# Second FFN of a one-layer diffusion block: gate and up as a 2x2 block product with seven products in place of eight

## The chip, the cores and the metric

One core of one Trainium2 chip runs the whole layer as a single launch. Every time is in device microseconds. A run's time is that of one execution; the profile comes from one execution of its own, and its clock starts with the span. The five engines work through instruction lists of their own, in order, and meet through semaphores: PE (TensorE, matmuls into PSUM; PEld are its weight loads), DVE (VectorE), ACT (ScalarE), POOL (GpSimd) and SP, which here only issues DMAs.

## What is computed

The layer takes 1024 latent tokens and 256 context tokens of width 1024. It is a half-step SwiGLU, a mixer (latent attention beside a state-space scan) and a second half-step SwiGLU, then a final RMSNorm. The change touches the second SwiGLU, which runs on the latent tokens alone:

```python
def swiglu(h, w_gu, w_down):
    gate, up = jnp.split(h @ w_gu, 2, axis=-1)
    return (jax.nn.silu(gate) * up) @ w_down
...
x = x + mx[5] * mix_x
x = x + 0.5 * mx[8] * swiglu(modulate(x, g_ffn2[l], mx[6], mx[7]), w_gu2[l], w_down2[l])
return rmsnorm(x, g_final)
```

`w_gu2` is 1024 x 5632 (gate and up, 2816 columns each), `w_down2` is 2816 x 1024.

## The kernel before

All matrix products are made in three passes: each operand is split into a rounded high part H (ACT copies it to the matmul type) and a remainder L (DVE or POOL subtracts), and `mm3` (L621 to L623) issues H·H, H·L and L·H into one PSUM bank. A matmul is 128 x 128 weights against 512 columns.

`mix_out_ffn2` (L1564) first makes the mixer's output projection, token tile by token tile (eight of 128), and then calls `ffn`. `ffn` walks f over 22 slices of 128 hidden columns. The 1024 tokens form two blocks of 512, `hT[0]` and `hT[1]`, kept transposed (eight k tiles of 128 on partitions). In step f it makes gate of both blocks (2 x 24 matmuls, tag `gu`), then the down product of slice f-1 (eight token tiles x two halves x 3 matmuls = 48, tag `dn`), each half added by DVE to the residual stream `acc` (L62, a helper that records every tensor_tensor), then up of both blocks (2 x 24). SiLU (L720) is ACT's, the product with up is DVE's, its split ACT's and POOL's. So a step has 144 matmuls and 16 additions of a PSUM bank to `acc`.

PSUM has four banks for `gu` and four for `dn`. Weights come by SP's queue (L663): gate and up of a slice are 128 x 1024 each, down 128 x 1024; they share four raw buffers. DVE multiplies down by the broadcast gate `g8`, ACT and POOL split all three (1024 wide). The order of work on every engine is the order in which the code is written; nothing reorders it. With `joint`, the down products of the last two slices are held back and made together, tile by tile, six matmuls into a bank; after each tile comes its share of the final norm: sum of squares on ACT, `rstd` (DVE, then a power on POOL), a scaled copy on DVE and the store.

The first slice's gate and up weights are loaded and split during the projection (L1690 to L1697). The normed tokens of block 1 (`xn`, tiles 4 to 7) are ready only after the last projection tile; their transposes (`trans(1, ...)` through `hook`) run between the matmuls of f = 0 on block 0.

Of the kernel before, what the change touches and what calls it, by code (L numbers as in the profile page):

```python
# [7 lines left out]
F32 = mybir.dt.float32  # L8
F32R = mybir.dt.float32r
# [38 lines left out]
class Kernel:  # L48
# [1515 lines left out]
    def mix_out_ffn2(self, sbig):  # L1564
        nc, a, acc = self.nc, self.a, self.acc
        B2 = [(0, 4), (4, 4)]
        with ExitStack() as st:
# [3 lines left out]
            P = {"w": w2}  # L1571
            xp = self.pool(st, "xn", bufs=4)
            with ExitStack() as s1:
# [113 lines left out]
                pre0 = {}  # L1687
                for t in range(2, NX):
                    if t in (2, 4):
                        which = t // 2 - 1  # L1690
                        wr = sm.tile([128, D], F32, tag="wor", name="w2r")
                        nc.sync.dma_start(wr, a["w_gu2"][0, which].rearrange("p k f -> p (k f)"))
                    if t in (3, 5):
                        pre0[0, which] = [tuple(w2.tile([128, 1024], F32R, tag=f"w{x}{which}", name=f"w{x}{which}")
                                                for x in "HL")]
                        self.split(wr, *pre0[0, which][0], nc.gpsimd)
# [11 lines left out]
            P["sg"], P["nsg"] = self.pool(st, "sg2"), 3  # L1708
            fin = self.pool(st, "fin2")
            g8 = fin.tile([128, D], F32, name="g8")  # L1710
            gf = fin.tile([128, D], F32, name="gf")
            self.gate_bc(g8, (8, 0))
            nc.sync.dma_start(gf, a["g_final"].to_broadcast([128, D]))
            P["gates"] = [(g8, P["act"])]
            out = self.out.rearrange("(j s) d -> j s d", s=NX)

            def hook(b):
                todo = list(range(KT if b else 0))

                def pre(kt):  # L1720
                    while todo and todo[0] <= kt + 2:
                        trans(1, todo.pop(0), "dn")
                return pre

            down = self.ffn(B2, hT, a["w_gu2"], a["w_down2"], acc, P, hook, preload=pre0, keep=True, joint=True)
            S = {}

            def post(t, cs, p):
                self.tt(acc[t][:, cs], p, acc[t][:, cs], ADD)

            def final(t):
                R = self.rstd(S.pop(t), D, "n")
                for q in range(2 if t == NX - 1 else 1):
                    cs = slice(q * 512, q * 512 + 512) if t == NX - 1 else slice(0, D)
                    self.stt(J[t][:, cs], acc[t][:, cs], R, gf[:, cs], MUL, MUL)
                    nc.sync.dma_start(out[:, t, cs], J[t][:, cs])

            J = {}
            for t in range(NX):
                down([t], post)  # L1740
                J[t] = xp.tile([128, D], F32, tag="xn", name="j")
                S[t] = self.sumsq(acc[t], J[t], "n")
                if t:
                    final(t - 1)
            final(NX - 1)


# [77 lines left out]
```

## Time and profile before

| what | value |
|---|---|
| three timed runs | 2544.89, 2546.02 (median), 2550.65 us |
| the profiled execution's own time | 2544.01 us |
| its span | 2542.2 us |
| PE busy in the span | 2427.4 us (95%) |
| DVE / ACT / POOL busy | 1434.2 / 816.1 / 1036.1 us |
| second FFN in the span | about 1803 to 2542 us |

How to read it: rows of the timeline give the start, the time from the first start to the last end, the engine, the line, the operation with output and inputs, a count, and in brackets the idle time before them with what ended it. Busy matmuls overlap (each is shown 0.39 us long, but one starts every 0.23 us), so a rate is taken from starts. PEclk is the granted TensorE clock, 1.00 at 2.4 GHz and 0.50 at 1.2 GHz.

### The profile page before, as it was taken

How to read it: one execution, taken by the hardware profiler on the slowest of the kernel's cores; microseconds unless marked ns; L12 is line 12 of the kernel's file. 1: busy time of each engine (PE TensorE's matmuls, PEld its weight loads, DVE VectorE, ACT ScalarE, POOL GpSimd, SP SyncE). 2: the span in 40 equal slices, each digit the busy share in tenths (PEclk: the TensorE clock that was granted, in tenths of full speed). 3: DMA queues.
4: the chain of work that ended last, by engine and by line, in shares of the span. 5: the costliest groups of instructions: out<-in, count | busy, mean ns of one | idle time of the engine just before them, and what ended most of it. 6: DMA issues, size and time to landing. Idle time of an engine off the chain costs nothing. (4 is left out here: it accounts for less than half of the span.)

```text
span 2542.2 us, 31980 instructions
## 1 busy us (share of the span) xinstructions
PE 2427.4 (95%) x12100; PEld 2004.9 (79%) x12100; DVE 1434.2 (56%) x2480; ACT 816.1 (32%) x1570; POOL 1036.1 (41%) x947
## 2 busy tenths in 40 slices
PE   7999998999999999898999999999999999999998
PEld 4788777888888887787777777777788888888886
DVE  3667578345434537747788888863344444444443
ACT  4311211211121112533677777762411111111112
POOL 2422314433433333426576666755433223323222
PEclk9999999999999999899999999999999999999999
DMA  7234621222222123316000000113211111111111
GB/s 283 86 106 135 205 83 38 71 70 59 75 71 71 57 79 126 123 38 192 23 17 4 14 14 25 38 66 126 75 44 49 50 50 50 50 45 46 50 42 67
DMA packets 83544, 185.14 MB, mean 73 GB/s; under 512 B 22199, under 2 KB 41911, under 8 KB 82366
## 3 DMA queue, kind: packets, MB, share of 16 engines
q1 hardware_dynamic: 59990, 163.93, 19.3%
q10 hardware_dynamic: 23400, 19.16, 2.6%
q8 instruction: 95, 1.56, 0.3%
q14 instruction: 59, 0.48, 0.1%
HBM read 155.52 MB, written 27.54 MB: 72 GB/s over the span
## 5 line engine op out<-in xcount | busy, mean ns | idle before, releaser
L62 POOL TENSOR_TENSOR wL<-raw,wH 128x1024 fp32r<-128x1024 f32 x130 | 313.8, 2418 | 787.6 <-ACT wH L616 776.5
L62 DVE TENSOR_TENSOR acc<-dn,acc 128x512 f32<-128x512 f32 x516 | 350.4, 690 | 352.3 <-PE dn L623 352.1
L621 PE MATMUL gu<-big,wH 128*128 128x512 f32 (+1 forms) x1056 | 379.9, 360 | 3.0 <-ACT sg L720 1.5
L623 PE MATMUL gu<-big,wL 128*128 128x512 f32 (+1 forms) x1056 | 374.8, 355 | 2.3 <-POOL wL L62 2.3
L622 PE MATMUL gu<-big,wH 128*128 128x512 f32 (+1 forms) x1056 | 374.6, 355 | 1.8 <-POOL big L62 1.8
L621 PE MATMUL dn<-wH,aH 128*128 128x512 f32 x792 | 314.6, 397 | 18.9 <-DVE acc L62 14.1
L623 PE MATMUL dn<-wH,aL 128*128 128x512 f32 x792 | 311.3, 393 | 1.0 <-POOL aL L62 1.0
L622 PE MATMUL dn<-wL,aH 128*128 128x512 f32 x792 | 311.4, 393 | 0.0
L616 ACT ACTIVATE wH<-raw 128x1024 fp32r<-128x1024 f32 x130 | 136.3, 1055 | 497.9 <-DVE raw L62 226.5
L62 DVE TENSOR_TENSOR sg<-gu,sg 128x512 f32<-128x512 f32 (+1 forms) x110 | 69.8, 635 | 391.7 <-PE gu L623 369.6
L622 PE MATMUL gu<-hL,wH 128*128 128x512 f32 x704 | 274.5, 390 | 4.3 <-POOL hL L62 3.0
L621 PE MATMUL gu<-hH,wH 128*128 128x512 f32 x704 | 274.6, 390 | 0.0
L623 PE MATMUL gu<-hH,wL 128*128 128x512 f32 x704 | 273.9, 389 | 0.0
L62 POOL TENSOR_TENSOR aL<-sg,aH 128x512 fp32r<-128x512 f32 (+1 forms) x110 | 140.4, 1277 | 277.5 <-ACT aH L616 275.0
L621 PEld LDWEIGHTS gu<-big,wH 128*128 128x128 f32 x1056 | 200.1, 189 | 36.0 <-issue 4.1
L623 PEld LDWEIGHTS gu<-big,wL 128*128 128x128 f32 x1056 | 199.9, 189 | 31.5 <-POOL wL L62 3.4
L622 PEld LDWEIGHTS gu<-big,wH 128*128 128x128 f32 x1056 | 200.1, 189 | 31.1 <-POOL big L62 2.2
L616 ACT ACTIVATE aH<-sg 128x512 fp32r<-128x512 f32 (+1 forms) x110 | 64.7, 589 | 461.6 <-DVE sg L62 425.0
L621 PEld LDWEIGHTS dn<-wH,aH 128*128 128x128 f32 x792 | 150.5, 190 | 54.4 <-DVE acc L62 15.8
L62 DVE TENSOR_TENSOR ptL<-pt,ptH 128x512 fp32r<-128x512 f32 x240 | 162.8, 686 | 52.2 <-ACT ptH L1417 51.7
L623 PEld LDWEIGHTS dn<-wH,aL 128*128 128x128 f32 x792 | 150.6, 190 | 33.6 <-POOL aL L62 1.4
L622 PEld LDWEIGHTS dn<-wL,aH 128*128 128x128 f32 x792 | 150.9, 191 | 31.1 <-issue 0.5
(317 smaller groups left out, 4635.7 us busy)
## 6 DMA issues: line engine op xcount, KB each, us to landing
raw<-in_w_gu SPq DMA_DIRECT2D x86, 512.0 KB, 3.4
wmr<-in_w_mod SPq DMA_DIRECT2D x56, 512.0 KB, 4.5
raw<-in_w_down SPq DMA_DIRECT2D x44, 512.0 KB, 3.3
row<-d_s SPq DMA_DIRECT2D x16, 576.0 KB, 4.0
wm<-in_w_mod SPq DMA_DIRECT2D x8, 1024.0 KB, 7.1
d_s<-T ACTq DMA_DIRECT2D x32, 160.0 KB, 2.7
ck<-d_s SPq DMA_DIRECT2D x16, 320.0 KB, 4.0
acc<-in_x SPq DMA_DIRECT2D x8, 512.0 KB
```

Source lines behind the costliest of these rows:

```text
L62: (eng or self.nc.vector).tensor_tensor(out=out, in0=a, in1=b, op=op)
L616: self.nc.scalar.activation(out=H, in_=raw, func=AF.Copy)
L621: mm(out, lhsT=AH, rhs=BH, start=start, stop=False)
L622: mm(out, lhsT=AH, rhs=BL, start=False, stop=False)
L623: mm(out, lhsT=AL, rhs=BH, start=False, stop=stop)
```

## The change

For one slice f the products of gate and up form a 2x2 block product. The four weight blocks are A11 and A12 (gate weights, k tiles 0-3 and 4-7) and the blocks a21 and A22 (up weights, the same halves). The four token blocks are B11 and B21 (block 0, k tiles 0-3 and 4-7; they are `hT[0]`) and B12 and B22 (block 1). Seven products of 12 matmuls each (four k tiles x three passes) take the place of eight: A11·B11, A12·B21, S1·T1, S2·T2, S3·T3, S4·B22 and A22·T4. S1 to S4 are sums of weight blocks, made anew for each slice by DVE (`Products.add`); T1 to T4 are sums of token blocks, made once in f = 0 (`part`). The seven banks are combined by DVE into gate and up of both blocks, in four scratch halves of `acc[8]` and `acc[9]` (P1, U2, U3, C22).

The new `ffn2` has a loop of its own. A step's order on PE is A11, S2, S3, S1, the down product of f-1, A12, A22, S4. The sums for slice f+1 and the splits of A11, S2, S3, S1 stand ahead of the down product, those of A12, A22, S4 at the step's end, followed by the loads of gate and up for f+2 (`load_gu`) and of down for f (`load_wd`, with its product by `g8` and its split). Raw buffers are single. The last down product is made alone, not together with the one before.

In the diff, some lines are left out, among them the removed body and the variant of `add` for slice 0 (`sums`), which runs in three parts during projection tiles 3, 4 and 5.

```diff
-            P = {"w": w2}
-            xp = self.pool(st, "xn", bufs=4)
+            raw1 = self.pool(st, "raw1")
+            sx = ExitStack()
+            xp = self.pool(sx, "xn", bufs=4)
+            ops = Products(self, w2)
...
+                    if t == 2:
+                        wr = [sm.tile([128, D], F32, tag="wor", name="w2r"), raw1.tile([128, D], F32, tag="r", name="w2r")]
+                        for which in range(2):
+                            nc.sync.dma_start(wr[which], a["w_gu2"][0, which].rearrange("p k f -> p (k f)"))
+                    if t == 3:
+                        prep = ops.sums(*wr, xp.tile([128, 512], F32, tag="hf", name="s", bufs=2))
+                    if t in (3, 4, 5):
+                        next(prep, None)
...
-                hB = self.pool(st, "hT2b", side="right")
-                hT.append(tuple(hB.tile([128, KT, 512], F32R, name=f"h{x}1") for x in "HL"))
-            P["act"] = P["wd"] = self.pool(st, "act2", bufs=2)
-            P["raw"] = self.pool(st, "raw2", bufs=4)
...
+
+    def ffn2(self, st, sx, h0, ops, raw1, xp, XN):
...
+        B["B11"], B["B21"] = (tuple(h[:, k:k + 4, :] for h in h0) for k in (0, 4))
...
+        def product(p, op, k):
+            (H, L), (bH, bL) = ops[op], B[pair[op]]
+            ks = slice(k * 128, (k + 1) * 128)
+            self.mm3(p, H[:, ks], L[:, ks], bH[:, k, :], bL[:, k, :], k == 0, k == 3)
+
+        def whole(op):
+            p = self.bank("gu", op)
+            for k in range(4):
+                product(p, op, k)
+            return p
+
+        def part(k, tt):
+            f = []
+            for kt, pool, tag in ((k, xp, "hf"), (k + 4, tt, "b22")):
+                t = self.bank("dn", "tp")
+                for i in range(4):
+                    nc.tensor.transpose(t[:, i * 128:(i + 1) * 128], XN[4 + i][:, kt * 128:(kt + 1) * 128], self.ident)
+                x = pool.tile([128, 512], F32, tag=tag, name=tag, bufs=2)
+                nc.scalar.activation(out=x, in_=t, func=AF.Identity, scale=av[:, kt:kt + 1], bias=bv[:, kt:kt + 1])
+                f.append(x)
+            b12, b22 = f
+            t1, t2, t3, t4 = (tt.tile([128, 512], F32, tag=f"t{i}", name=f"t{i}") for i in range(4))
+            g = lambda x, i: B[x][i][:, k, :]
+            fp = lambda x, i: g(x, i).bitcast(F32)
+            self.tt(t1, fp("B11", 0), fp("B11", 1), ADD)
+            self.tt(t4, fp("B21", 0), fp("B21", 1), ADD)
+            self.tt(t1, b12, t1, SUB)
+            self.split(t1, g("T1", 0), g("T1", 1), nc.gpsimd)
+            self.tt(t2, b22, t1, SUB)
+            self.split(t2, g("T2", 0), g("T2", 1), nc.gpsimd)
+            self.tt(t3, b22, b12, SUB)
+            self.split(t3, g("T3", 0), g("T3", 1))
+            self.tt(t4, t4, t2, SUB)
+            self.split(t4, g("T4", 0), g("T4", 1))
+            self.split(b22, g("B22", 0), g("B22", 1), nc.gpsimd)
+
+        wd, act = {}, {}
+        W = {}
+
+        def load_gu(f):
+            if f < NF:
+                r = [raw1.tile([128, D], F32, tag="r", name="rg"), W["raw"].tile([128, D], F32, tag="r", name="ru")]
+                for i in range(2):
+                    nc.sync.dma_start(r[i], a["w_gu2"][f, i].rearrange("p k f -> p (k f)"))
+                W[f] = r
+
+        def load_wd(f):
+            r = W["raw"].tile([128, D], F32, tag="wd", name="wdr")
+            nc.sync.dma_start(r, a["w_down2"][f])
+            self.tt(r, r, g8, MUL)
+            H, L = (W["act"].tile([128, D], F32R, tag=f"wd{x}", name=f"wd{x}") for x in "HL")
+            self.split(r, H, L, nc.gpsimd)
+            wd[f] = (H, L)
+
...
+        def down(f, tiles):
+            for t in tiles:
+                aH, aL = act[f][t // 4]
+                ts = slice((t % 4) * 128, (t % 4 + 1) * 128)
+                for half in range(2):
+                    cs = slice(half * 512, half * 512 + 512)
+                    p = self.bank("dn", "dn")
+                    self.mm3(p, aH[:, ts], aL[:, ts], wd[f][0][:, cs], wd[f][1][:, cs], True, True)
+                    self.tt(acc[t][:, cs], p, acc[t][:, cs], ADD)
+
...
+        for f in range(NF):
+            P1, U2, U3, C22 = tmp
+            if f == 0:
+                with ExitStack() as s1:
+                    tt = self.pool(s1, "tt")
+                    p1, p2 = (self.bank("gu", x) for x in ("A11", "A12"))
+                    for i, (p, op) in enumerate(((p1, "A11"), (p2, "A12"))):
+                        for k in range(2):
+                            part(2 * i + k, tt)
+                            product(p, op, 2 * k)
+                            product(p, op, 2 * k + 1)
+                sx.close()
+                W["act"] = self.pool(st, "act2")
+                W["raw"] = self.pool(st, "raw2")
+                g8 = self.pool(st, "fin2").tile([128, D], F32, name="g8")
+                self.gate_bc(g8, (8, 0))
+                load_gu(1)
+            else:
+                p1 = whole("A11")
+            nc.scalar.copy(P1, p1)
+            self.tt(U2, whole("S2"), P1, ADD)
+            self.tt(U3, whole("S3"), U2, ADD)
+            p = whole("S1")
+            self.tt(C22, p, U3, ADD)
+            self.tt(U2, p, U2, ADD)
+            if f + 1 < NF:
+                ops.add(*W[f + 1], temps)
+                for x in ("A11", "S2", "S3", "S1"):
+                    ops.split(x)
+            if f:
+                down(f - 1, range(NX))
+                p2 = whole("A12")
+            self.tt(P1, p2, P1, ADD)
+            nc.scalar.activation(out=P1, in_=P1, func=AF.Silu)
+            self.tt(U3, whole("A22"), U3, ADD)
+            self.tt(P1, P1, U3, MUL)
+            act[f] = [split_act(0, P1)]
+            self.tt(U2, whole("S4"), U2, ADD)
+            nc.scalar.activation(out=U2, in_=U2, func=AF.Silu)
+            self.tt(U2, U2, C22, MUL)
+            act[f].append(split_act(1, U2))
+            if f + 1 < NF:
+                for x in ("A12", "A22", "S4"):
+                    ops.split(x)
+            load_gu(f + 2)
+            load_wd(f)
+
+        gf = W["raw"].tile([128, D], F32, tag="wd", name="gf")
+        nc.sync.dma_start(gf, a["g_final"].to_broadcast([128, D]))
+        out = self.out.rearrange("(j s) d -> j s d", s=NX)
...
+        def final(t):
+            R, J = self.rstd(S.pop(t), D, "n"), acc[8 + t % 2]
+            for q in range(2 if t == NX - 1 else 1):
+                cs = slice(q * 512, q * 512 + 512) if t == NX - 1 else slice(0, D)
+                self.stt(J[:, cs], acc[t][:, cs], R, gf[:, cs], MUL, MUL)
+                nc.sync.dma_start(out[:, t, cs], J[:, cs])
+
+        for t in range(NX):
+            down(NF - 1, [t])
+            S[t] = self.sumsq(acc[t], acc[8 + t % 2], "n")
+            if t:
+                final(t - 1)
+        final(NX - 1)
...
+    def add(self, g, u, temp):
+        k, half = self.k, lambda x, i: x[:, i * 512:(i + 1) * 512]
+        s = self.src
+        s["A11"], s["A12"], a21, s["A22"] = half(g, 0), half(g, 1), half(u, 0), half(u, 1)
+        s["S1"] = temp()
+        k.tt(s["S1"], a21, s["A22"], ADD)
+        s["S2"] = temp()
+        k.tt(s["S2"], s["S1"], s["A11"], SUB)
+        s["S3"] = a21
+        k.tt(a21, s["A11"], a21, SUB)
+        s["S4"] = temp()
+        k.tt(s["S4"], s["A12"], s["S2"], SUB)
+
+    def split(self, x):
+        self.t[x] = tuple(self.pool.tile([128, 512], F32R, tag=x + y, name=x + y) for y in "HL")
+        self.k.split(self.src.pop(x), *self.t[x], self.k.nc.gpsimd)
```

SP's queue in the middle of the loop, before. Each row is one load into a `raw` buffer: gate, up and down of `w_gu2` and `w_down2`.

```order
L663 DMA raw_20035<-in_w_gu2 128x1024
L663 DMA raw_20095<-in_w_gu2 128x1024
L663 DMA raw_20181<-in_w_down2 128x1024
L663 DMA raw_20248<-in_w_gu2 128x1024
L663 DMA raw_20308<-in_w_gu2 128x1024
L663 DMA raw_20394<-in_w_down2 128x1024
```

And now (L1760 is `load_gu`, L1765 `load_wd`):

```order
L1760 DMA rg_17698<-in_w_gu2 128x1024
L1760 DMA ru_17699<-in_w_gu2 128x1024
L1765 DMA wdr_17702<-in_w_down2 128x1024
L1760 DMA rg_17935<-in_w_gu2 128x1024
L1760 DMA ru_17936<-in_w_gu2 128x1024
L1765 DMA wdr_17939<-in_w_down2 128x1024
```

Before, four raw buffers took the loads in turn. Now the down weights of a step (`wdr`) stand right behind the gate (`rg`) and up (`ru`) weights of the step after next, each into a buffer of its own kind.

DVE around the down product, before. `raw` is the down weights times `g8`, `sg` the product of SiLU and up, `dn` a bank of the down product; 16 rows of that kind stand there, of which the last of one step and the first two of the next are shown.

```order
L62 TENSOR_TENSOR acc_68<-dn_20602,acc_68 128x512
L62 TENSOR_TENSOR raw_20607<-raw_20607,g8_16424 128x1024
L62 TENSOR_TENSOR sg_20492<-gu_20614,sg_20492 128x512
L62 TENSOR_TENSOR sg_20519<-gu_20644,sg_20519 128x512
L62 TENSOR_TENSOR acc_68<-dn_20740,acc_68 128x512
L62 TENSOR_TENSOR acc_68<-dn_20745,acc_68 128x512
```

And now. S4, S2, S3, S1 and dn are PSUM banks, `acc<-acc` is SiLU times up, `wdr` the down weights times `g8`, the four rows from `s_18003` on are the weight sums of the next slice.

```order
L62 TENSOR_TENSOR acc_68<-S4_17903,acc_68 128x512
L62 TENSOR_TENSOR acc_68<-acc_68 128x512
L62 TENSOR_TENSOR wdr_17939<-wdr_17939,g8_16624 128x1024
L62 TENSOR_TENSOR acc_68<-S2_17960,acc_68 128x512
L62 TENSOR_TENSOR acc_68<-S3_17974,acc_68 128x512
L62 TENSOR_TENSOR acc_68<-S1_17988,acc_68 128x512 x2
L62 TENSOR_TENSOR s_18003<-ru_17936 128x512
L62 TENSOR_TENSOR s_18005<-s_18003,rg_17935 128x512
L62 TENSOR_TENSOR ru_17936<-rg_17935,ru_17936 128x512
L62 TENSOR_TENSOR s_18008<-rg_17935,s_18005 128x512
L62 TENSOR_TENSOR acc_68<-dn_18026,acc_68 128x512
L62 TENSOR_TENSOR acc_68<-dn_18031,acc_68 128x512
```

Between the last product of one step and the first `dn` bank of the next, DVE now has the product of the down weights, the evacuations of three `gu` banks and four weight sums to do; before, it went from `sg` straight to `dn`.

DVE after the last normed token tiles (`xn`), where block 1 is transposed and f = 0 begins, before:

```order
L66 TENSOR_SCALAR xn_16400<-acc_68,rr_16335 128x1024
L66 TENSOR_SCALAR xn_16402<-acc_68,rr_16398 128x1024
L62 TENSOR_TENSOR raw_16428<-raw_16428,g8_16424 128x1024
L62 TENSOR_TENSOR hL1_16409<-hf_16481,hH1_16408 128x512
L66 TENSOR_SCALAR hf_16493<-tp_16487,ma20_2466,col60_2289 128x512
L62 TENSOR_TENSOR hL1_16409<-hf_16505,hH1_16408 128x512
L66 TENSOR_SCALAR hf_16517<-tp_16511,ma20_2466,col60_2289 128x512
L62 TENSOR_TENSOR sg_16460<-gu_16462,sg_16460 128x512
```

And now. `t0` to `t3` are the token sums of one `part`, T3L and T4L the remainders that DVE makes itself; `hf` and `b22` come from ACT.

```order
L66 TENSOR_SCALAR xn_16428<-acc_68,rr_16363 128x1024
L66 TENSOR_SCALAR xn_16430<-acc_68,rr_16426 128x1024
L62 TENSOR_TENSOR t0_16467<-hH0_15659,hL0_15660 128x512
L62 TENSOR_TENSOR t3_16470<-hH0_15659,hL0_15660 128x512
L62 TENSOR_TENSOR t0_16467<-hf_16458,t0_16467 128x512
L62 TENSOR_TENSOR t1_16468<-b22_16465,t0_16467 128x512
L62 TENSOR_TENSOR t2_16469<-b22_16465,hf_16458 128x512
L62 TENSOR_TENSOR T3L_16445<-t2_16469,T3H_16444 128x512
L62 TENSOR_TENSOR t3_16470<-t3_16470,t1_16468 128x512
L62 TENSOR_TENSOR T4L_16447<-t3_16470,T4H_16446 128x512
```

Where two operations stood for a pair of transposed k tiles, eight stand for a pair now, in four parts one after the other.

## Rows read from the trace of the kernel before

**Rows 1.** Windows of the loop: length, busy per engine (instructions), PEclk, DMA share, GB/s

```profile
2000.00:2100.00 100.00, 100.00 (x443) 82.81 (x442) 40.23 (x57) 16.51 (x22) 31.23 (x17) 1.00 0.14 48
```

**Rows 2.** Timeline of PE: first matmul of a down product, first one behind it

```profile
2106.48 0.39 PE L621 MATMUL dn<-wH,aH 128*128 128x512 f32 x1
...
2117.36 0.39 PE L621 MATMUL gu<-hH,wH 128*128 128x512 f32 x1
```

**Rows 3.** Timeline of DVE, one step of the loop

```profile
2107.36 10.89 DVE L62 TENSOR_TENSOR acc<-dn,acc 128x512 f32<-128x512 f32 x16 [10.80 <-PE dn L623]
2118.17 1.22 DVE L62 TENSOR_TENSOR raw<-raw,g 128x1024 f32<-128x1024 f32 x1
2123.07 0.69 DVE L62 TENSOR_TENSOR sg<-gu,sg 128x512 f32<-128x512 f32 x1 [3.68 <-PE gu L623]
...
2140.00 5.45 DVE L62 TENSOR_TENSOR acc<-dn,acc 128x512 f32<-128x512 f32 x8 [10.80 <-PE dn L623]
```

**Rows 4.** Timeline of ACT in the same step: splits 512 and 1024 wide

```profile
2129.24 0.63 ACT L616 ACTIVATE aH<-sg 128x512 fp32r<-128x512 f32 x1 [4.81 <-DVE sg L62]
2129.78 1.04 ACT L616 ACTIVATE wH<-raw 128x1024 fp32r<-128x1024 f32 x1
```

**Rows 5.** Timeline of POOL there: remainders 512 and 1024 wide

```profile
2129.95 1.29 POOL L62 TENSOR_TENSOR aL<-sg,aH 128x512 fp32r<-128x512 f32 x1 [4.16 <-ACT aH L616]
2131.19 2.40 POOL L62 TENSOR_TENSOR wL<-raw,wH 128x1024 fp32r<-128x1024 f32 x1
```

**Rows 6.** What SP's queue waited for, 1800 to 2543 us: total, times, longest

```profile
SPq L663 <- POOL wL L62: 630.3, 60, 17.5
```

**Rows 7.** DMA issues by line: count, size, median us from issue to landing

```profile
raw<-in_w_down SPq DMA_DIRECT2D x44, 512.0 KB, 3.3
```

**Rows 8.** Timeline of SP where several loads are issued together

```profile
1803.42 0.32 SPq L792 DMA_DIRECT2D g<-d_gate  x1
...
1804.26 0.43 SPq L663 DMA_DIRECT2D raw<-in_w_down  x1
1804.74 1.76 SPq L663 DMA_DIRECT2D raw<-in_w_gu  x3
```

**Rows 9.** Timeline of DVE: end of xn, first down weights, last product of f = 0

```profile
1809.15 0.75 DVE L66 TENSOR_SCALAR xn<-acc,rr 128x1024 f32<-128x1024 f32 x1 [0.44 <-POOL rr L62]
1810.50 1.23 DVE L62 TENSOR_TENSOR raw<-raw,g 128x1024 f32<-128x1024 f32 x1 [0.60 <-DMA raw<-in_w_down]
...
1834.75 0.69 DVE L62 TENSOR_TENSOR sg<-gu,sg 128x512 f32<-128x512 f32 x1 [7.69 <-PE gu L623]
```

**Rows 10.** Timeline of DVE: remainders with both inputs in SBUF

```profile
1784.79 0.69 DVE L62 TENSOR_TENSOR hL<-hf,hH 128x512 fp32r<-128x512 f32 x1 [1.19 <-ACT hf L611]
...
1786.79 1.39 DVE L62 TENSOR_TENSOR hL<-hf,hH 128x512 fp32r<-128x512 f32 x1 [0.53 <-ACT hf L611]
```

**Rows 11.** Timeline of POOL at the same place

```profile
1786.35 1.29 POOL L62 TENSOR_TENSOR hL<-hf,hH 128x512 fp32r<-128x512 f32 x1 [2.12 <-DVE hf L66]
```

**Rows 12.** Timeline of DVE: last slice and final norm

```profile
2509.31 0.69 DVE L62 TENSOR_TENSOR sg<-gu,sg 128x512 f32<-128x512 f32 x1 [4.76 <-PE gu L623]
2510.60 0.69 DVE L62 TENSOR_TENSOR acc<-dn,acc 128x512 f32<-128x512 f32 x1 [0.60 <-PE dn L623]
...
2515.29 0.14 DVE L66 TENSOR_SCALAR rv<-ss 128x1 f32<-128x1 f32 x1
...
2518.50 0.14 DVE L66 TENSOR_SCALAR rv<-ss 128x1 f32<-128x1 f32 x1
```

**Rows 13.** Timeline of PE in the first FFN: matmuls behind two idle stretches

```profile
424.06 0.79 PE L621 MATMUL dn<-wH,aH 128*128 128x512 f32 x1 [7.59 <-DVE acc L62]
...
1018.17 0.50 PE L621 MATMUL dn<-wH,aH 128*128 128x512 f32 x1 [2.80 <-DVE gp L62]
```

**Rows 14.** Windows at these two places

```profile
424.00:428.00 4.00, 3.94 (x9) 3.13 (x10) 3.67 (x11) 0.00 (x0) 0.00 (x0) 0.50 0.00 0
...
1019.00:1020.00 1.00, 1.00 (x4) 0.81 (x3) 0.97 (x2) 0.00 (x0) 1.00 (x1) 0.50 0.20 78
```

More of the change, by code (lines that the diff above doesn't have):

```diff
@@ L1685, in pre @@
                         z_T(t // 2 + 1)
-                pre0 = {}
                 for t in range(2, NX):
[L1689 to L1696, printed above, removed]
+                    if t == 2:
[6 more added lines that the diff above has]
+                        next(prep, None)
                     part(t, range(8), lambda k: pre(t, k))
@@ L1703, in mix_out_ffn2 @@
                 sbig.close()
-                hB = self.pool(st, "hT2b", side="right")
-                hT.append(tuple(hB.tile([128, KT, 512], F32R, name=f"h{x}1") for x in "HL"))
-            P["act"] = P["wd"] = self.pool(st, "act2", bufs=2)
-            P["raw"] = self.pool(st, "raw2", bufs=4)
[L1708 to L1745, printed above, removed]
+            self.ffn2(st, sx, hT[0], ops, raw1, xp, XN)
+    def ffn2(self, st, sx, h0, ops, raw1, xp, XN):
+        nc, a, acc = self.nc, self.a, self.acc
+        hB = self.pool(st, "hT2b", side="right")
+        names = ("B22", "T1", "T2", "T3", "T4")
+        B = {x: tuple(hB.tile([128, 4, 512], F32R, name=f"{x}{y}") for y in "HL") for x in names}
+        B["B11"], B["B21"] = (tuple(h[:, k:k + 4, :] for h in h0) for k in (0, 4))
+        pair = {"A11": "B11", "S2": "T2", "S3": "T3", "S1": "T1", "A12": "B21", "A22": "T4", "S4": "B22"}
+        tmp = [acc[8 + i // 2][:, (i % 2) * 512:(i % 2) * 512 + 512] for i in range(4)]
+        av, bv = self.mod[2, 0]
+        def product(p, op, k):
[46 more added lines that the diff above has]
+            wd[f] = (H, L)
+        def temps():
+            return W["raw"].tile([128, 512], F32, tag="s", name="s", bufs=3)
+        def down(f, tiles):
[7 more added lines that the diff above has]
+                    self.tt(acc[t][:, cs], p, acc[t][:, cs], ADD)
+        def split_act(b, x):
+            r = tuple(W["act"].tile([128, 512], F32R, tag=f"a{y}{b}", name=f"a{y}{b}") for y in "HL")
+            self.split(x, *r, nc.gpsimd)
+            return r
+        for f in range(NF):
[47 more added lines that the diff above has]
+        out = self.out.rearrange("(j s) d -> j s d", s=NX)
+        S = {}
+        def final(t):
[10 more added lines that the diff above has]
+        final(NX - 1)
@@ new lines, with __init__, __getitem__, sums @@
+class Products:
+    def __init__(self, k, pool):
+        self.k, self.pool, self.src, self.t = k, pool, {}, {}
+    def __getitem__(self, x):
+        return self.t[x]
+    def add(self, g, u, temp):
[13 more added lines that the diff above has]
+        self.k.split(self.src.pop(x), *self.t[x], self.k.nc.gpsimd)
+    def sums(self, g, u, t):
+        s, k = self.src, self.k
+        half = lambda x, i: x[:, i * 512:(i + 1) * 512]
+        s["A11"], s["A12"], a21, s["A22"] = half(g, 0), half(g, 1), half(u, 0), half(u, 1)
+        k.tt(t, a21, s["A22"], ADD)
+        s["S1"] = s["S2"] = s["S4"] = t
+        self.split("S1")
+        k.tt(t, t, s["A11"], SUB)
+        self.split("S2")
+        yield
+        k.tt(a21, s["A11"], a21, SUB)
+        s["S3"] = a21
+        self.split("S3")
+        self.split("A11")
+        yield
+        k.tt(t, s["A12"], t, SUB)
+        for x in ("S4", "A12", "A22"):
+            self.split(x)
```

## The prediction

> **What bounds the kernel now.** I read the windows of the loop first. PE is busy 100 us of 100 at a granted clock of 1.00 [rows 1]; DVE works 40, POOL 31, ACT 17. Then I take PE's pace from starts, not from its shown durations: the 48 matmuls of a down product start at 2106.48 and the next group at 2117.36 [rows 2], 10.88/48 = 0.2267 us each. A step has 144, so 32.6 us, and the step measured from one down product to the next on DVE is 2140.00 - 2107.36 = 32.64 [rows 3]. So the loop is PE work without a gap, and only what takes matmuls away, or what makes PE wait, moves its time. Next I look at how near the others are. During the down product DVE adds 16 banks in 10.89 us [rows 3], each 0.69 long against PE's 0.68 a bank: here DVE keeps up with nothing to spare, and only the four dn banks (2.72 us of PE work) lie between them. Last, SP: its weight loads waited 630 us in 60 places for POOL to give a buffer back [rows 6]. The loads come early enough because there are buffers, and an issue that waits holds up all issues behind it.
>
> I count in the profiled execution, 2544.0 us (span 2542.2); the median of the runs is 2.0 higher.
>
> **What the change removes.** Twelve matmuls of 144 in each of 22 steps: 264 x 0.2267 = 59.8 us of PE work. A step is then 132 x 0.2267 = 29.9. This is what the change could gain if PE still never waited.
>
> **The loop, step by step.** Let T be the start of A11 of the next step, right behind S4. I follow what must happen before that step's down product, one operation behind the other, with the durations of [rows 3 to 5] (DVE 0.69, ACT 0.63 and POOL 1.29 for 512 columns, pitch of POOL 1.24; some 0.05 for a hand-over). The SiLU and the copy of P1 I take as one ACT operation of 0.6 to 0.63, by the 512-wide split [rows 4].
> - S4's bank to U2 ends at T+1.0, SiLU 1.65, product 2.35, high part 3.0, remainder aL 4.35 on POOL. Behind it in POOL's list stand the remainders A12 (to 5.6) and A22 (6.85).
> - These two release the single raw buffers. SP issues gate and up for f+2 at 5.6 and 6.9, and only then, in the same queue, the down weights of f, at about 7.3. Nothing else holds them; they are simply third in line.
> - They land 3.3 us after issue when alone [rows 7]. Where a down load was issued at 1804.26 behind two broadcasts of its size and ahead of three more loads [rows 8], DVE got it at 1810.50 [rows 9], 6.2 us after issue. Here two are ahead of it, one of them well under way. Between 3.3 and 6.2 I take 4.3, nearer the lone load: T+11.6.
> - DVE, in order, waits for it with the product by g8: to 12.85 (1.22 [rows 3]). ACT's high part ends at 13.95 (1.04 [rows 4]), POOL's remainder at 16.4 (2.40 [rows 5]). PE has by then done A11, S2, S3, S1 (4 x 2.72 = 10.88) and stands from T+10.9 to 16.5, but for one matmul with the high part.
> - The wait has a queue behind it. On DVE these are U2, U3, C22, U2 (they also need ACT's copy of P1, which stands behind the high part, to 14.6): 4 x 0.69, to 17.3. Then the four weight sums, and only then the first dn bank. A sum reads two SBUF operands, and such a DVE operation took 0.69 alone but 1.39 beside a POOL remainder that ran at the same time [rows 10, 11]: it ended 0.5 after POOL's. POOL is in A11's remainder until 17.7, so the sums (0.63 each, back to back) end near 20.2.
> - PE fills the four dn banks by 19.2 and waits for the first to be emptied, at 20.9. Then 12 banks at 0.68 end at 29.1, and A12, A22, S4 (8.16) at 37.2.
> - The clock: after 7.59 us of idle PE came back at half clock and did 9 matmuls in 4 us in place of 17.7 [rows 13, 14], 2 us lost; after 2.80 us it also fell, to 0.50 [rows 13, 14]. Here the loss falls on the four banks that would wait for DVE anyway (16.5 + 2.72 + 2.0 = 21.2 against 20.9), so it costs 0.3.
>
> So a step takes 37.5, against 32.64: +4.9. That holds for 20 steps; for the last two no gate and up weights are loaded, and the down weights come early. 20 x 4.9 = **+98**. Bounds: landing 3.3 and no turn lost to POOL 35.6 (+59); landing 6.2 and one more turn of 1.3 40.7 (+161). I stay in the middle because the load is behind two others, not five.
>
> A rule of the Trainium skill bears on the sums (SBUF — State Buffer, "Who interferes with whom"): a VectorE instruction with two SBUF inputs and a GpSimd one that reads SBUF shut each other out for a whole instruction. The trace agrees in rows 10 and 11, with 1.39 for 0.69; by the rule taken strictly every sum could lose a turn to POOL, which is the upper bound above; without it the sums would end 0.6 earlier.
>
> **The start, f = 0.** Today the last xn ends at 1809.9 and f = 0's last matmul at 1834.5 (its product starts at 1834.75, 0.27 later) [rows 9]: 24.6 us. Now block 1 needs four parts in a row, each with eight DVE operations on SBUF operands (5.5 us), three POOL remainders (3.9) and seven ACT operations, of which two lie in DVE's chain: 6.4 us a part where DVE and POOL overlap, 9.7 where they take turns. S2 can end only with T2 of the last part, 24 to 35 us after xn, then come S3, S1, A22, S4 (10.9) and a rest of 0.45: 35.4 to 46.5. Rows 10 and 11 speak for turns; I take 43: **+18** (11 to 22). The products of A11 and A12 hide in it. The sums and splits for slice 0 lie in the projection, whose PE work covers them: POOL has 1.4 us more ahead of one group of splits there; I cost it at nothing (1 us if not).
>
> **The last slice and the end.** The down product of slice 20, until now part of the joint one, is made in step 21: 29.9 against 96 matmuls, 21.8: **+8.2**. Now the last product of the loop is S4 of step 21, and the first dn bank is added 7.9 us behind it (aL 4.35, then the down remainder to 7.1, 0.8 for a bank), where today it is 2510.60 - 2509.04 = 1.6 behind the last up matmul (2509.31 less 0.27) [rows 12]. From there the end is DVE's pace, 3.21 us a tile (2515.29 to 2518.50) [rows 12], joint or not; the first four banks come at 0.68 in place of 1.36, so 2.0 are won: 7.9 - 1.6 - 2.0 = **+4.3**. PE's 96 matmuls of the joint product lay under that pace, so halving them buys little.
>
> Sum: 98 + 18 + 8 + 4 = +128, 2544 + 128 = 2672; with the 2.0 of the median **2674 us**, 5.0% slower.
>
> **Rivals.**
> - *The clock is paid in full.* PE returns late by 2.0 us in each step, if the clock falls in the second wait (for DVE) rather than the first, or twice. For it: a fall after only 2.80 us [rows 13, 14]. Against it: DVE's lateness covers it. Price 20 x 1.9 on top: 2712. The Trainium skill says this of loops that wait for a transfer in each pass (TensorE: Matmul & The Clock Gate, "HAM oscillation — how this bites in real kernels"): the clock falls in every one of them. The rows above agree that it falls; whether it costs here is decided by DVE.
> - *The down weights are not late.* Then the wait at g8 is gone and the next limit shows: C22 and U2 after S1 (T+12.5), sums to 15.0, PE's second wait to 15.7, then 16.3 of work: 32.0 a step, -0.6. 2544 - 12 + 18 + 8 + 4 + 2 = 2564. For it: loads in this loop are prompt today. Against: the queue order and the chain to A22's remainder, each link with a measured length.
> - *PE stays fed, and it is faster.* One mechanism: the four dn banks absorb all that DVE does ahead of them. Then 29.9 a step: -54 + 30 + 2 gives 2522. It decides at a step of 31.1, where 20 steps pay for the 30 us of start and end, that is, if DVE reaches its first dn bank by T+14.1. By the sum it gets there at 20.2, with prompt weights at 15.0. Against it is the DVE row with no room [rows 3].
>
> **How the numbers follow.** The forecast (2625 to 2710) has 0.65, the full clock price 0.20, weights not late 0.08, PE fed 0.05, no change 0.02. Of the forecast's own range the low end is 2544 + 11 + 59 + 12 + 2 = 2628, and the high end, 2544 + 22 + 161 + 13 + 2 = 2742, needs all bounds at once; 2610 to 2725 holds most of the first two cases and leaves out 0.2. A measurement here can tell 0.2% (5 us) from nothing: faster 0.05, same 0.03, slower 0.92.
>
> **What would show it.** In the profile of the changed kernel: a step of 36 to 39 us with PE busy some 80% of it; PE's first down matmul with a low part (`wdL`) waiting 2 us or more for POOL, each step; DVE idle some 9 us ahead of the product by `g8`, ended by the DMA of the down weights; SP's down load issued right behind up's, 7 us after A11's start; granted clock below 1.00 in the loop; f = 0 ending 35 to 47 us after the last xn. It is wrong if that DMA ends no wait on DVE, or if the step is below 32.6.

## The result and the profile after

| | before | after |
|---|---|---|
| device time, median (range), us | 2547.3 (2544.9 to 2550.7) | 2725.6 (2722.8 to 2727.7) |
| span of the profiled execution, us | 2542.2 | 2721.0 |
| mean granted clock | 0.990 | 0.951 |

The changed kernel takes 1.070 times the time of the kernel before (95% interval 1.068 to 1.072): 178 us more. The prediction had 2674 with a range to 2725. The direction was right, and so was the mechanism, a PE that stands in each step because the down weights come late. The size was 52 us short (51 between the two profiled spans), and the time lies just beyond the range.

Windows of the changed kernel, columns as in [rows 1]: a stretch of the loop, and within a step the 4.9 us behind PE's wait.

```profile
2000.00:2400.00 400.00, 337.07 (x1341) 268.74 (x1340) 208.79 (x311) 80.77 (x133) 143.59 (x104) 0.89 0.12 40
...
2235.10:2240.00 4.90, 4.90 (x12) 3.84 (x13) 4.87 (x9) 1.75 (x3) 2.77 (x3) 0.50 0.00 2
```

PE was busy 100 us of 100 at a clock of 1.00 [rows 1]. Now it is busy 84% at 0.89. A step, from one copy of P1 to the next on ACT (1918.17 to 2430.41, 13 steps), is 39.40 us, against 32.64 before [rows 3] and 37.5 predicted.

One step follows, itself 39.91 us long. T, the start of A11, is 2217.01. First SP's queue, then DVE, then PE (each as its timeline has it: start, length, engine, line, operation, and in brackets the idle time ahead and what ended it).

```profile
2222.69 0.33 SPq L1760 DMA_DIRECT2D rg<-in_w_gu  x1
2223.94 0.33 SPq L1760 DMA_DIRECT2D ru<-in_w_gu  x1
2224.32 0.42 SPq L1765 DMA_DIRECT2D wdr<-in_w_down  x1
```

```profile
2230.28 1.23 DVE L62 TENSOR_TENSOR wdr<-wdr,g 128x1024 f32<-128x1024 f32 x1 [10.99 <-DMA wdr<-in_w_down]
2233.16 2.88 DVE L62 TENSOR_TENSOR acc<-S,acc 128x512 f32<-128x512 f32 x4 [1.65 <-ACT acc L1808]
2235.95 0.86 DVE L62 TENSOR_TENSOR s<-ru 128x512 f32<-128x512 f32 x1
...
2238.66 2.48 DVE L62 TENSOR_TENSOR acc<-dn,acc 128x512 f32<-128x512 f32 x4
2241.43 8.22 DVE L62 TENSOR_TENSOR acc<-dn,acc 128x512 f32<-128x512 f32 x12 [0.29 <-PE dn L623]
```

```profile
2217.01 0.39 PE L621 MATMUL A<-hH,A11H 128*128 128x512 f32 x1
...
2232.65 0.79 PE L621 MATMUL dn<-wdH,aH 128*128 128x512 f32 x1 [4.60 <-ACT wdH L616]
2235.08 0.80 PE L622 MATMUL dn<-wdL,aH 128*128 128x512 f32 x1 [1.64 <-POOL wdL L62]
```

The down load is issued at T+7.31, third in line, as predicted (7.3). DVE has the weights at T+13.27, where 11.6 was predicted. From there the predicted chain runs at the predicted lengths: PE's first matmul with `wdL` at T+18.07, DVE's first dn bank at T+21.65, 8.38 behind the weights (predicted: 8.6). The page of the changed kernel says how long these loads took (last number, us from issue to landing, the median of the five or six loads of each kind whose landing the trace has), and how long DVE waited for the down weights in all. Over the 20 steps DVE starts on the down weights 6.06 us after their issue on average (5.6 to 6.7).

```profile
L62 DVE TENSOR_TENSOR wdr<-wdr,g 128x1024 f32<-128x1024 f32 x22 | 26.9, 1225 | 221.8 <-DMA wdr<-in_w_down 221.8
...
wdr<-in_w_down SPq DMA_DIRECT2D x22, 512.0 KB, 5.8
rg<-in_w_gu SPq DMA_DIRECT2D x21, 512.0 KB, 3.4
ru<-in_w_gu SPq DMA_DIRECT2D x21, 512.0 KB, 5.0
```

Where the 178.8 us between the two spans lie, each stage cut at the same event in both traces:

| stage | before | after | more | predicted |
|---|---|---|---|---|
| to the end of the last `xn` | 1809.9 | 1812.8 | 2.9 | 0 |
| f = 0: to the end of its last matmul | 24.6 | 47.7 | 23.1 | 18 |
| 20 steps, f = 1 to 20 | 652.8 | 790.9 | 138.1 | 98 |
| the last step | 21.8 | 29.9 | 8.1 | 8.2 |
| from the last product to the end | 33.2 | 39.7 | 6.5 | 4.3 |

(The 20 steps run from A11 of f = 1 at 1860.55 to A11 of f = 21 at 2651.43; the first of them is 42.1 long, since the down weights of f = 0 come later still.)

### The profile page after: what moved, and what is told of

It is laid out like the page before. It is cut to its first block, busy times and chain, and to the rows that moved or that the text cites. A ratio compares the mean times of both kernels' runs of the same rounds, so it can differ in the third digit from the quotient of the medians.

```text
span 2721.0 us, 32118 instructions
## 1 busy us (share of the span) xinstructions
PE 2440.8 (90%) x11836; PEld 1993.6 (73%) x11836; DVE 1618.1 (59%) x2762; ACT 880.1 (32%) x1718; POOL 1141.5 (42%) x1065
## 5 line engine op out<-in xcount | busy, mean ns | idle before, releaser
L62 POOL TENSOR_TENSOR wL<-raw,wH 128x1024 fp32r<-128x1024 f32 x66 | 160.6, 2441 | 430.2 <-ACT wH L616 430.2
L621 PE MATMUL dn<-wdH,aH 128*128 128x512 f32 x352 | 161.9, 460 | 107.3 <-ACT wdH L616 101.6
L621 PE MATMUL dn<-wH,aH 128*128 128x512 f32 x440 | 177.7, 404 | 17.8 <-DVE acc L62 13.7
L622 PE MATMUL dn<-wdL,aH 128*128 128x512 f32 x352 | 159.7, 454 | 34.6 <-POOL wdL L62 34.6
L621 PEld LDWEIGHTS dn<-wdH,aH 128*128 128x128 f32 x352 | 78.5, 223 | 138.0 <-ACT wdH L616 110.4
L623 PE MATMUL dn<-wH,aL 128*128 128x512 f32 x440 | 174.8, 397 | 1.3 <-POOL aL L62 1.3
L622 PE MATMUL dn<-wL,aH 128*128 128x512 f32 x440 | 175.0, 398 | 0.0
L616 ACT ACTIVATE wH<-raw 128x1024 fp32r<-128x1024 f32 x66 | 69.0, 1058 | 273.2 <-PE dn L623 120.7
L623 PE MATMUL dn<-wdH,aL 128*128 128x512 f32 x352 | 154.4, 439 | 0.0
L1417 ACT CAST ptH<-pt 128x512 fp32r<-128x512 f32 x240 | 138.4, 586 | 46.7 <-PE pt L1414 42.3
```

The lines of the kernel that those rows point to most:

```text
L62: (eng or self.nc.vector).tensor_tensor(out=out, in0=a, in1=b, op=op)
L616: self.nc.scalar.activation(out=H, in_=raw, func=AF.Copy)
L621: mm(out, lhsT=AH, rhs=BH, start=start, stop=False)
L622: mm(out, lhsT=AH, rhs=BL, start=False, stop=False)
L623: mm(out, lhsT=AL, rhs=BH, start=False, stop=stop)
L1417: nc.scalar.copy(H, p)
```

## The experiments

Each starts from the changed kernel. Steps are means between copies of P1, 13 or 14 steps. Beside the experiments the kernel before took 2545.8 to 2546.8 us.

**The down load ahead of the others.** Issued ahead of gate and up, from where its product and split are made as before:

```diff
+            wdr = fetch_wd(f)
             load_gu(f + 2)
-            load_wd(f)
+            load_wd(f, wdr)
```

> One edit to the changed kernel: the DMA of the down weights of f is issued ahead of the two gate and up loads of f+2 instead of behind them; its buffer is free since the remainder wdL of the step before. Theory A (the queue order makes the down weights late, and that is the larger part of the step's 39.4 us): the step loses the 10 to 11 us that DVE waits for the DMA, and what binds next is the four weight sums ahead of the first dn bank: 32 us a step if the clock stays up, 34 to 35 if PE's shorter wait (some 2 us) also drops it; 2722 - 20 x 7.4 - 5 = 2569, or 2615 to 2630 with the clock. Theory B (the chain of products and remainders binds, not the DMA): the DMA's wait goes and the step stays above 37; 2670 or more.

2598.4 us (ratio 1.021, 1.019 to 1.022): 127 us won back by the order of three DMA issues. A step is 33.05. DVE no longer waits for the load. SP's queue around one down load, and DVE's product with it:

```profile
2200.02 0.33 SPq L1760 DMA_DIRECT2D ru<-in_w_gu  x1
2203.63 0.33 SPq L1765 DMA_DIRECT2D wdr<-in_w_down  x1
2232.40 0.33 SPq L1760 DMA_DIRECT2D rg<-in_w_gu  x1
```

```profile
2228.75 1.22 DVE L62 TENSOR_TENSOR wdr<-wdr,g 128x1024 f32<-128x1024 f32 x1
```

The load gains more than its place behind two transfers. It no longer stands behind issues that wait for the remainders A12 and A22, so it goes out one step earlier, when POOL's `wdL` has freed its buffer. That is 25.12 us ahead of DVE's product, and its time to landing no longer counts.

Two more answers from this trace: what PE waited for (1900 to 2500 us: total, times, longest), and the windows of two steps.

```profile
PE dn L621 <- DVE acc L62: 32.2, 18, 1.8
```

```profile
2160.88:2192.92 32.04, 30.25 (x134) 24.70 (x133) 19.64 (x30) 7.88 (x13) 14.12 (x11) 1.00 0.16 50
2226.55:2260.20 33.65, 31.86 (x134) 25.85 (x133) 20.26 (x30) 7.88 (x13) 14.11 (x11) 0.95 0.14 47
```

PE now waits for DVE, whose first dn bank comes at T+14.8; the second rival had put it at T+15.0 and the step at 32.0. The 1 us above that in the mean is the clock: the 19 steps behind the first are of two lengths, six of 32.0 at a clock of 1.00, as in the first window, and 13 of 33.6 at 0.95, as in the second. Theory A held, between its two figures.

**One load ahead instead of two.** In `load_gu` the down load stands between the two:

```diff
                 for i in range(2):
                     nc.sync.dma_start(r[i], a["w_gu2"][f, i].rearrange("p k f -> p (k f)"))
+                    if i == 0 and mid is not None:
+                        wd[mid] = fetch_wd(mid)
```

> One edit to the changed kernel: the DMA of the down weights stands between gate's and up's load instead of behind both; sums and splits as in the changed kernel. It tells what part of the landing (5.9 us) is the sharing with two loads ahead. Theory A (each load ahead costs about 1 us or more): issued 1.2 us sooner and landing in 4.5 to 5 us, so that DVE has the weights 2.2 to 2.6 us sooner and the step is as much shorter: 2722 - 20 x 2.4 = 2674. Theory B (the landing doesn't depend on the loads ahead): only the issue is sooner, 2722 - 24 = 2698.

2682.2 us (1.054, 1.052 to 1.055), a step of 37.18. DVE waited 2.2 us less for the weights in a step like the one shown (8.80 for 10.99), and the mean step is 2.2 shorter. Over the 20 steps of each kernel DVE's mean wait is 8.7 for 11.1, and the load is 4.9 us from issue to DVE's start for 6.1. Its DVE row, then how long the load took to landing (median, last number) in this kernel, and third the same in the experiment before it:

```profile
2214.46 1.23 DVE L62 TENSOR_TENSOR wdr<-wdr,g 128x1024 f32<-128x1024 f32 x1 [8.80 <-DMA wdr<-in_w_down]
```

```profile
wdr<-in_w_down SPq DMA_DIRECT2D x22, 512.0 KB, 4.5
```

```profile
wdr<-in_w_down SPq DMA_DIRECT2D x21, 512.0 KB, 3.5
```

So the same 512 KB land in 3.5 us when the last load was issued 3.6 us ahead, in 4.5 behind one load issued just ahead and in 5.8 behind two: 1.0 and 1.3 us for each. (These are medians of five or six landings. In the other experiments with two loads just ahead they are 5.6 to 6.4, so the second step is 1.1 to 1.9.) The result lies between the two theories' figures, nearer to A. The Trainium skill (DMA: Bandwidth & Descriptors, "Anatomy of one DMA — SWDGE (gpsimd) path") counts 436 GB/s for the part of a transfer that grows with its bytes; it says so of GpSimd's path, and these loads are SP's. By an estimate from that page of the Trainium skill 512 KB are 1.2 us, and the two differences agree with it to 0.2.

**Does DVE hold the step, or the clock?** Three kernels. In the first the sums and the splits behind them move from ahead of the down product to behind A12's evacuation; in the second 30 matmuls, which nobody reads, fill PE's wait; the third has both.

```diff
-            if f + 1 < NF:
-                ops.add(*W[f + 1], temps)
-                for x in ("A11", "S2", "S3", "S1"):
-                    ops.split(x)
             ...
             self.tt(P1, p2, P1, ADD)
+            if f + 1 < NF:
+                ops.add(*W[f + 1], temps)
+                for x in ("A11", "S2", "S3", "S1"):
+                    ops.split(x)
```

```diff
             self.tt(U2, p, U2, ADD)
+            if f:
+                p = self.bank("dn", "warm")
+                for _ in range(30):
+                    nc.tensor.matmul(p, lhsT=ops["S1"][0][:, 0:128], rhs=B["T1"][0][:, 0, :], start=True, stop=True)
```

> One edit to the changed kernel: the four weight sums on DVE, and the splits of A11, S2, S3, S1 behind them, stand after the evacuation of A12 instead of ahead of the first dn bank. Down weights stay late. Theory A (PE's restart at half clock and DVE's late start are level with each other, so that taking away either gives little): 2715 to 2722, within 0.3% of the changed kernel. Theory B (as the prediction had it: DVE's sums hold PE after the restart and the clock is hidden under them): the step gets shorter by 20.9 - 18.8 = 2 us, 2680.

> One addition to the changed kernel: 30 matmuls more in each step (into a dn bank that nobody reads; 30 x 0.227 = 6.8 us), behind S1, where PE stands and waits for the down weights. Nothing else is moved. They keep the clock up. Theory A (clock and DVE's late start are level): DVE's first dn bank at T + 21.7 then sets the end: a step of 38.5 against 39.4, 2722 - 18 = 2704. Theory B (the clock alone, 3 us in each step, is what was missed): 2722 - 20 x 3 = 2660. Theory C (the clock is hidden, as the prediction had it): no change, 2722.

> Both edits at once: the sums after A12's evacuation, and the 30 extra matmuls. Theory A (level): now both are gone and the step is wdL at T + 18.1, 47 matmuls 10.7 and 8.2: 36.9; 2722 - 20 x 2.5 = 2672, far more than the two single edits together. Theory B (clock alone): as the run with the matmuls alone, 2660.

Measured: 2754.9, 2722.5 and 2724.2 us; steps of 40.92, 38.88 and 39.11 (changed kernel: 2725.6, 39.40).

The extra matmuls restore the clock, and little follows: these steps are 0.5 us shorter, all 20 together 8 us, and the last step, where PE has no wait to fill, takes 6.8 of them back (36.7 for 29.9). From that kernel's trace, one step's window, and PE in it, with the four dn banks full:

```profile
2215.19:2254.20 39.01, 37.31 (x164) 30.25 (x162) 19.93 (x30) 7.90 (x13) 13.99 (x11) 1.00 0.13 41
```

```profile
2237.75 0.50 PE L621 MATMUL dn<-wdH,aH 128*128 128x512 f32 x1 [1.54 <-DVE acc L62]
```

With the clock at 1.00 PE waits 1.54 us for DVE instead. So the clock costs about 0.5 us a step in the changed kernel, though 12 of its matmuls ran at 0.50. That lies between theory A (0.9) and theory C (hidden); theory B, that the clock alone had been missed (3), fell.

The moved sums gave neither figure: the kernel got slower by 29 us. Its trace says why (DVE, then POOL, then SP; T is 2231.48 here):

```profile
2211.69 0.69 DVE L62 TENSOR_TENSOR acc<-dn,acc 128x512 f32<-128x512 f32 x1 [0.30 <-PE dn L623]
2212.97 0.69 DVE L62 TENSOR_TENSOR acc<-dn,acc 128x512 f32<-128x512 f32 x1 [0.59 <-PE dn L623]
...
2233.72 1.66 DVE L62 TENSOR_TENSOR acc<-acc 128x512 f32<-128x512 f32 x1 [0.70 <-ACT acc L1827]
```

```profile
2231.83 1.74 POOL L62 TENSOR_TENSOR S1L<-s,S1H 128x512 fp32r<-128x512 f32 x1
2233.54 1.28 POOL L62 TENSOR_TENSOR aL<-acc,aH 128x512 fp32r<-128x512 f32 x1
```

```profile
2238.77 0.33 SPq L1760 DMA_DIRECT2D rg<-in_w_gu  x1
```

The remainders of the moved splits, and behind them aL, now stand beside DVE's two products, and both take longer (1.77 us and, shown, 1.66 in place of 0.69). The chain to A12L is longer, gate's load goes out at T+7.29 in place of T+5.68, and the down weights behind it are 1.6 us later: 20 x 1.6 = 32 us, which covers the 29 lost: 39.40 + 1.6 = 41.0 for the 40.92 measured. By this difference the sums' own move is worth 0.1. The rows of DVE say why: it waits for PE in the first banks, 1.28 apart at half clock, so that with DVE's delay gone the clock binds. The third kernel keeps the clock up as well in most steps, still with the loads 1.6 later, and its step is 1.8 shorter than the first's. (Of the 19 steps behind the first, four are at 0.96 and 40.4 to 40.7 long, the others at 1.00 and 37.8 to 40.2.) So DVE's delay and the clock cover each other: alone they are worth 0.1 and 0.5 us, together some 2. Ahead of both stands the load.

**Load early and sums moved.** Both edits, `fetch_wd` ahead and the sums behind A12:

> Two edits to the changed kernel: the DMA of the down weights ahead of the loads of gate and up, and the weight sums behind the evacuation of A12. Theory A (with the load early, the sums are the next limit, and behind them POOL's row aL, A12L, A22L, S4L, wdL, which in the run with the sums moved is 1.6 us later): wdL ends at T + 12.1, PE stands 1.2 us at the start of the down product and then runs through: 31.1 a step, 2722 - 20 x 8.3 - 5 = 2551; 2575 if the wait drops the clock. Theory B (something else holds the step, DVE's pace in the 16 additions): not below 32.6, 2580 or more.

2567.4 us (1.008, 1.006 to 1.010), a step of 31.28. What PE waited for, 1900 to 2500 us:

```profile
PE dn L622 <- POOL wdL L62: 20.2, 19, 1.1
```

That is the wait that theory A named, behind three remainders on POOL, at about the length it gave (1.2). The clock stays at 1.00 in these steps, and DVE's first dn bank comes at T+13.1. The time lies between theory A's two figures.

**PE fed.** In addition the down split goes ahead of those three:

```diff
+            load_wd(f, fetch_wd(f))
             if f + 1 < NF:
                 for x in ("A12", "A22", "S4"):
                     ops.split(x)
-            wdr = fetch_wd(f)
             load_gu(f + 2)
-            load_wd(f, wdr)
```

> As the run before it, and the down weights' product and split stand ahead of the splits of A12, A22 and S4, so that wdL no longer waits behind three remainders on POOL. Theory A (then nothing makes PE wait in a step): 132 x 0.2267 = 29.9 us a step, PE without a gap, clock 1.00 in the loop; 2722 - 20 x 9.5 - 5 = 2527, faster than the kernel before by 0.7%. Theory B (the 36 added operations of DVE, ACT and POOL cost some PE time anyway): 31 to 32 a step, 2550 to 2570.

2535.6 us (0.996, 0.995 to 0.998). A window of its loop:

```profile
2000.00:2400.00 400.00, 400.00 (x1767) 331.34 (x1766) 294.72 (x406) 102.02 (x170) 191.37 (x131) 1.00 0.17 55
```

PE is busy 400 us of 400 at a clock of 1.00, and a step is 29.91, which is 132 x 0.2267. So Strassen's saving (seven products for eight) is real, all of it, once nothing is late: 2.7 us a step. The kernel gains only 10 us, since the stages around the loop still cost more.

The down load of this kernel, DVE's product with it, and the time to landing from the page:

```profile
2208.41 0.42 SPq L1765 DMA_DIRECT2D wdr<-in_w_down  x1
```

```profile
2230.55 1.21 DVE L62 TENSOR_TENSOR wdr<-wdr,g 128x1024 f32<-128x1024 f32 x1
```

```profile
wdr<-in_w_down SPq DMA_DIRECT2D x22, 512.0 KB, 6.4
```

It goes out 0.37 us behind up's, as in the changed kernel, and lands in 6.4 us, later than there. It costs nothing, because it is issued 22.14 us ahead of its use: what was won is the step in which the load is issued, not the time it takes.

**Is it PE's work again?** The same kernel with 12 unread matmuls more in each step, as many as the identity saves (the edit of the second kernel above, with 12 for 30):

> The version with the early down weights, the sums behind A12 and the down remainder first (29.92 us a step), with 12 matmuls more behind S1 in each step, into a dn bank that nobody reads: as many as Strassen's identity saves. In the changed kernel 30 more cost nothing. Theory A (PE is the bound again): 12 x 0.2267 = 2.72 us a step, 21 steps: 2535.6 + 57 = 2593, in place of the gain. Theory B (the step is held by another engine at nearly the same pace): less than 30 us more.

2590.9 us, a step of 32.63, as the kernel before. Theory A held: 12 matmuls cost 2.72 us a step here, while 30 cost nothing in a step of the changed kernel that has the wait.

**The parts of f = 0.** On top of the fed kernel, all remainders there on DVE, behind the sums of their part:

```diff
-            self.split(t1, g("T1", 0), g("T1", 1), nc.gpsimd)
...
-            self.split(b22, g("B22", 0), g("B22", 1), nc.gpsimd)
+            for x, v in (("T1", t1), ("T2", t2), ("T3", t3), ("T4", t4), ("B22", b22)):
+                self.split(v, g(x, 0), g(x, 1))
```

> As the run before it, and in the four parts of f = 0 the three remainders that POOL made are made by DVE, the sums all ahead of them. Theory A (DVE's and POOL's operations on SBUF operands take turns there, so that a part of 9.05 us is their sum): 11 DVE operations at 0.62 to 0.69 are 6.8 to 7.6 a part, 4 x 1.5 to 2.2 = 6 to 9 us less, 2518 to 2521. Theory B (no turns, the chain from part to part sets it): DVE does 3 operations more, 2 us a part longer, 2535.

2527.6 us (0.993, 0.991 to 0.994), the fastest version but for the next one, which can't be told from it. In the changed kernel a part's DVE and POOL rows read:

```profile
1844.24 0.98 DVE L62 TENSOR_TENSOR T3L<-t,T3H 128x512 fp32r<-128x512 f32 x1 [0.70 <-ACT T3H L616]
1845.15 1.74 DVE L62 TENSOR_TENSOR t<-t,t 128x512 f32<-128x512 f32 x1
```

```profile
1842.86 1.82 POOL L62 TENSOR_TENSOR T1L<-t,T1H 128x512 fp32r<-128x512 f32 x1 [2.49 <-ACT T1H L616]
1844.64 1.70 POOL L62 TENSOR_TENSOR T2L<-t,T2H 128x512 fp32r<-128x512 f32 x1
```

Both engines are slower beside each other (DVE 1.74 for 0.69, POOL 1.7 to 1.8 for 1.29), and a part is 9.05 us. With 11 operations on DVE and none on POOL it is 6.82 (T1L at 1830.76 and 1837.57): doing more on one engine is 2.2 us faster. The rule quoted in the prediction on two SBUF inputs beside GpSimd (the Trainium skill, SBUF — State Buffer, "Who interferes with whom") is borne out by these lengths, on both engines.

**The products of f = 0 beside its parts.** S2, S3, S1 and A22 slice by slice behind each part, A11 and A12 ahead of them:

```diff
+                    Q = {x: self.bank("gu", x) for x in ("S2", "S3", "S1", "A22")}
+                    for k in range(4):
+                        if k < 3:
+                            part(k + 1, tt)
+                        for x in Q:
+                            product(Q[x], x, k)
```

> The version with the early down weights, the sums behind A12, the down remainder first and DVE's remainders in f = 0 (2527.6), and in f = 0 the products S2, S3, S1 and A22 are made k slice by k slice behind each part, A11 and A12 whole ahead of them. Theory A (f = 0 is bounded by the parts, 6.8 us each, and the products behind the last part are 10.9 us of PE work of which 3/4 can lie beside the parts): about 7 us less, 2520. Theory B (the down weights of f = 0, whose buffer opens only when the parts' tiles close, are next): the gain is given back in the first down product, 2525 to 2528.

2525.4 us (0.991, 0.990 to 0.993): not distinguishable from the version before it. S4 of f = 0 ends 4 us sooner behind the start of the last `xn` (35.6 for 39.6), but the weights of f = 1, whose buffers open only when the parts' tiles close, are not there:

```profile
1852.93 1.30 DVE L62 TENSOR_TENSOR s<-ru 128x512 f32<-128x512 f32 x1 [3.61 <-DMA ru<-in_w_gu]
```

The first dn bank comes 54.1 us behind the start of the last `xn`, against 53.1. Theory B's time held, but not the load that it named: DVE waited for up's weights of f = 1, and had no wait for the down weights of f = 0.

## Why the prediction was short

- **The order of the queue: right.** Third in line at T+7.3, and the largest cost by far. Taken away, 127 us go.
- **The landing: the step that failed.** "Between 3.3 and 6.2 I take 4.3, nearer the lone load." It was 6.0 in the step shown and 6.06 on average over the 20. The row with a load behind others of its size [rows 8, 9], 6.2, was the nearer one; a load issued just ahead costs 1.0 to 1.3 us. With 7.3 + 6.06 for 11.6 this is 1.77 us of the 2.0 by which the 20 steps exceed the forecast on average, 20 x 1.77 = 35 of the loop's 40 and of the 51 us in all. The chain after it came out as forecast, so the mechanism was right and this term was too small.
- **DVE's chain behind the weights: right**, 8.38 for 8.6.
- **The clock in the loop: right in size (about 0.5 us for 0.3), by a thinner cover than thought.** The half clock itself lasted longer, 12 matmuls and more. The rival with the clock in full had 2712, the nearest total, by a mechanism that the run with the filled wait does not show: restoring the clock gave 0.5 us a step, where it needed 1.9. Its nearness is luck.
- **f = 0: 5 us short, above its own upper end (47.7 for 46.5).** The turns came as feared: the wait for the last T2L ends at 1846.40, 33.6 behind the last `xn`, where the forecast of 43 put it at 31.7; that is 1.9 of the 5. The rest is the clock, which was left out: the 13 matmuls from there took 5.7 us in place of 2.9. Here nothing covers it:

```profile
1843.66 0.79 PE L621 MATMUL S<-T2H,S2H 128*128 128x512 f32 x1 [5.09 <-ACT T2H L616]
1846.40 0.79 PE L622 MATMUL S<-T2L,S2H 128*128 128x512 f32 x1 [1.95 <-POOL T2L L62]
...
1847.42 0.63 PE L621 MATMUL S<-T3H,S3H 128*128 128x512 f32 x1
```

- **The projection: 2.9 where nothing was counted.** From the first `xn` to the last (starts) it is 69.1 us for 66.6. PE waited there (1740 to 1821 us) for DVE's scaling of `z`, a wait that the kernel before doesn't have:

```profile
PE zt L1592 <- DVE z L66: 2.2, 1, 2.2
```

  The weight sums for slice 0 are DVE's there, and I had looked at POOL alone. In the ten experiments the stretch is 69.1 to 70.8. No run took these sums out, so that they are the cause is read from the wait, not shown.
- **The last step: right (8.1 for 8.2). The end: 2.2 short.** The first dn bank came 8.3 us behind S4 for 7.9. The next came 1.28 and 1.16 apart in place of 0.68, because PE came back from its wait at half clock (1.1 us in all), and at the last tile DVE waits 0.7 for ACT's sum of squares. On DVE:

```profile
2689.64 0.69 DVE L62 TENSOR_TENSOR acc<-dn,acc 128x512 f32<-128x512 f32 x1 [4.88 <-PE dn L623]
2690.92 0.69 DVE L62 TENSOR_TENSOR acc<-dn,acc 128x512 f32<-128x512 f32 x1 [0.59 <-PE dn L623]
...
2715.57 0.15 DVE L66 TENSOR_SCALAR rv<-ss 128x1 f32<-128x1 f32 x1 [0.65 <-ACT acc L585]
```

- **The rival "PE stays fed": wrong for this kernel, right as a mechanism.** It put the deciding point at a first dn bank by T+14.1. With prompt weights and the sums ahead it was T+14.8 and the kernel slower. With the sums moved it was T+13.1, ahead of that point, and the kernel was still slower (2567.4), since its step, with PE's wait for `wdL`, was 31.28 (the prediction had 31.1 as the even point), and the stages around the loop cost more than the prediction's 30 us (41 in the changed kernel). With the down split first it was T+12.3 and the kernel faster.

- **The bounds: loosely worked.** The upper one has one more turn of 1.3 us, not a turn for every sum, as the sentence on the two SBUF inputs has it; and without a turn the sums would end 0.4 us earlier (17.3 + 4 x 0.63 = 19.8), not 0.6. In the step shown the first sum took 0.86 and the others 0.69 and 0.68.

The high bound of the sum, 2742, was itself cut to 2725 because it "needs all bounds at once". The landing near its bound would alone have given 2674 + 35 = 2709. The rest of the loop and f = 0 (5 us each), the projection (3) and the end (2), each of them small, were needed to pass 2725.

## What to carry to other kernels

Saving work on the engine that bounds a loop is worth nothing if the new order makes one transfer wait behind others in its queue; look first at what stands ahead of each DMA issue and from which engine's remainder its buffer comes free. When a load stands behind others, price it by a row of the trace in which it does so too, not by its lone landing time; or issue it so early that its landing doesn't count, as in the fed kernel. And two delays that cover each other show nothing when one of them is taken away: look for the event ahead of both.

## What was not expected of the hardware

- A 512 KB load took 3.5, 4.5 and 5.8 us to landing (medians) with none, one and two such loads issued within 1.7 us ahead of it; behind two it was 5.6 to 6.4 in the other experiments.
- DVE operations with two SBUF inputs took up to 1.77 us beside POOL remainders (0.69 alone), POOL's up to 1.82 (1.29 alone): more than the 1.39 of [rows 10].
- Behind a wait of 4.60 and one of 1.64 us PE ran its next 12 matmuls or more at half clock; 30 unread matmuls in that wait kept it at 1.00, at no cost where the wait was.
